# Six more weight granules in the seven-product stage ahead of attention

## The chip, the cores and the metric

One core of one Trainium2 chip runs the whole program. The metric is device time in microseconds of one execution; of several runs the median is given. A profile is one execution, and its times count from the first instruction of the program.

## The reference

The program computes one layer of a hybrid trunk: a half-step feed-forward, token mixing, another half-step feed-forward, over 512 latent and 128 context tokens (640 together) of width 1024. Only the mixing is touched:

```
mq, mk, mv, mo, mg, dq, dk, dv, gm, gd = split_cols(h @ w_in)   # nine projections 1024 wide, gates 16
att = diff_attention(rope(rmsnorm(dq)), rope(rmsnorm(dk)), dv)  # 8 heads, two softmaxes each
hm  = mlstm(mq * 256 ** -0.5, mk, mv, mg)                       # 4 heads of 256, two directions
hm  = rmsnorm(hm) * sigmoid(mo)
y   = sigmoid(gm) * (hm @ w_br_m) + sigmoid(gd) * (att @ w_br_d)
out = y @ w_out
```

Around each half step and the mixing stand modulations: rows of `silu(c) @ w_ada + b`, scaling and shifting the normed tokens and gating the residual.

## The kernel before

**Weights.** A projection 1024 wide is cut into four granules of 256 columns (1 MB each). Every fp32 weight and every activation is split into a high and a low part, and a product is three matmuls (high by high, high by low, low by high). A granule computed directly is four feature units (two column halves by two halves of 320 tokens, 24 matmuls of 320 columns each) or five token units (24 matmuls of 256 columns each).

**The seven-product stage.** `Winograd.products` computes a granule by seven products of half-size blocks in place of eight, 7 x 12 matmuls of 320 columns. ScalarE and VectorE prepare the weights one granule ahead: `parts` makes differences and splits wB and wC, `sums` splits the rest, ww. The order within a granule is A11, S1, the two last products of the granule before, S2, A12, S3. Four results come out per granule: two straight from a bank, two as a bank plus a copy that ScalarE made (`copy_of`). `Gates` runs this stage ahead of attention with six granules: three each of the branch gates gd and gm. Its callback `between(i, at)` does the work that rides along, at the start (0) or late (1) in granule i: the tables of the rotation and the rotation of the first queries and keys.

**Fills.** The other granules are fills. `Fill` holds a queue of granules in a fixed order; TensorE runs one unit of it where the program says so, and ScalarE and VectorE split the next weights. In attention a head has five query blocks. A block writes its scores to a single bank of PSUM, VectorE takes the minimum, ScalarE two exponentials, VectorE mixes the two softmaxes, TensorE transposes the mix in the next block and multiplies by the values. The table `UNITS` says for each head how many units stand in a block behind the transposes (first number) and behind the values (second), and at the head's end. Odd heads end with five further units. Behind the last head `drain(n)` runs units until n granules are left. In the memory stage `fill.pace(us, 1)` spreads the rest over the cells: each cell adds that many us to what is due, and a unit runs when more than 1.4 are due and takes 3.3 off; three units run ahead of the cells.

**Columns.** The 56 column tiles of the later modulations are `Columns`: a tile is a 512 KB load and two multiply-and-sum instructions of VectorE (L813). They ride along in several stages; the memory stage does 12, loaded through SP's queue (`load_columns_raw`).

**Order.** TensorE's instructions stay in the order of the program. On the other engines a planner orders them, except inside `written()`, where the order is that of the program too. DMA queues run in order.

## Time and profile before

| | |
|---|---|
| median of 3 runs | 1818.51 us (1817.56 to 1819.2) |
| span of the profiled execution | 1816.4 us; the page gives no other time for it |
| granted TensorE clock | 1.000 |
| TensorE, VectorE, ScalarE busy | 99%, 73%, 49% of the span |
| seven-product stage | from 505 to 578 us |
| attention | to 1056 us |
| memory stage | to about 1216 us |

In the profile PE is TensorE's matmuls, PEld its weight loads, DVE VectorE, ACT ScalarE, POOL GpSimd and SP the engine that issues most DMAs. A matmul's time is from its start to its modelled end; matmuls overlap, so their pace is read from start to start. ps_f are the banks of seven-product and feed-forward results, ps_p those of feature units, ps_t of token units, sc the scores.

### The profile page before, as it was taken

To read this page: it belongs to the slowest core of one execution; us is meant where nothing else is said; L and a number is where in the kernel's file an instruction comes from. 1 tells how busy PE (TensorE), PEld (TensorE's weight loads), DVE (VectorE), ACT (ScalarE), POOL (GpSimd) and SP (SyncE) were. 2 spreads that over 40 slices of the span, in tenths; PEclk is the share of its full clock that TensorE was granted. 3 is DMA by queue.
4 is the path that set the end of the run, shared out by engine and by line. 5 is a ranking of instruction groups with operands and counts; after the bars stand their busy time and mean duration, and the time that the engine had idled before them with its cause. 6 is when DMAs were issued, how large, how long until landed. Compare 5 with 4: busy or idle time off the path is not lost.

```text
span 1816.4 us, 30813 instructions
## 1 busy us (share of the span) xinstructions
PE 1793.6 (99%) x12622; PEld 1754.8 (97%) x12622; DVE 1323.8 (73%) x2140; ACT 894.8 (49%) x1558; POOL 37.1 (2%) x65
## 2 busy tenths in 40 slices
PE   9999999999999999999999999999999999999998
PEld 7999999999999999999999889999999999999998
DVE  6889986677886776475575649876767888897485
ACT  5654553333755454455465454674336545554432
POOL 0000000100000000000000000000000000000010
PEclk9999999999999999999999999999999999999999
DMA  8255566977244322112222055665652355657992
GB/s 330 106 197 183 185 224 235 344 228 257 82 138 159 106 76 78 63 63 89 80 89 72 20 169 163 223 254 183 238 170 80 134 172 185 202 181 275 352 307 83
DMA packets 130622, 307.69 MB, mean 169 GB/s; under 512 B 9841, under 2 KB 92017, under 8 KB 117553
## 3 DMA queue, kind: packets, MB, share of 16 engines
q1 hardware_dynamic: 120114, 263.64, 42.1%
q0 software_dynamic: 9680, 39.46, 6.7%
q8 instruction: 99, 1.62, 0.4%
q10 hardware_dynamic: 688, 2.63, 0.4%
q14 instruction: 41, 0.34, 0.1%
HBM read 238.14 MB, written 67.56 MB: 168 GB/s over the span
## 4 chain that ended last, share of the span: by engine, by line
PE 84%; DVE 7%; DMA 5%; ACT 3%; issue 1%; SPq 0%; DVEq 0%; ACTq 0%
PE ps_f L75 43%; PE ps_p L75 19%; PE ps_t L75 11%; PE sc L75 3%; PE ps_o L75 2%; DVE ww L54 2%; PE ps_n L75 2%; DMA raw<-in_w2b 2%; DMA raw_a<-in_w_ada_k 1%; PE ps_wT L78 1%; PE ps_u L75 1%; DVE junk L813 1%; PE ps_qkT L78 1%; DMA out_new_c<-Cn 1%; DMA P<-nm_dram 1%
## 5 line engine op out<-in xcount | busy, mean ns | idle before, releaser
L75 PE MATMUL ps_f<-S,ww 128*128 128x320 f32 x2184 | 352.5, 310 | 3.0 <-DMA S<-g_dram 1.0
L75 PEld LDWEIGHTS ps_f<-S,ww 128*128 128x128 f32 x2184 | 327.5, 188 | 7.0 <-DVE ww L54 4.6
L75 PE MATMUL ps_p<-hH,wH 128*128 128x320 f32 x672 | 212.4, 316 | 0.7 <-DVE stage L61 0.7
L75 PE MATMUL ps_p<-hH,wL 128*128 128x320 f32 x672 | 207.7, 309 | 0.0
L75 PE MATMUL ps_p<-hL,wH 128*128 128x320 f32 x672 | 207.7, 309 | 0.0
L54 DVE TENSOR_TENSOR ww<-raw,ww 128x2048 fp32r<-128x2048 f32 (+1 forms) x67 | 150.2, 2241 | 63.7 <-ACT ww L51 63.6
L75 PE MATMUL ps_f<-hm,ww 128*128 128x320 f32 x1176 | 185.8, 309 | 0.6 <-DVE ww L54 0.6
L75 PE MATMUL ps_t<-wH,hH 128*128 128x256 f32 x640 | 185.2, 289 | 0.9 <-DVE x L57 0.9
L75 PE MATMUL ps_t<-wH,hL 128*128 128x256 f32 x640 | 181.0, 283 | 0.9 <-DVE hL L54 0.9
L75 PE MATMUL ps_t<-wL,hH 128*128 128x256 f32 x640 | 180.8, 283 | 0.0
L75 PEld LDWEIGHTS ps_f<-hm,ww 128*128 128x128 f32 x1176 | 175.7, 188 | 1.2 <-DVE ww L54 1.2
L75 PE MATMUL ps_f<-hm,wB 128*128 128x320 f32 x1008 | 161.5, 309 | 0.0
L51 ACT ACTIVATE ww<-raw 128x2048 fp32r<-128x2048 f32 (+1 forms) x67 | 125.3, 1871 | 57.9 <-DVE raw L54 33.6
L75 PEld LDWEIGHTS ps_f<-hm,wB 128*128 128x128 f32 x1008 | 151.3, 188 | 0.0
L54 DVE TENSOR_TENSOR raw<-raw 128x1024 f32<-128x1024 f32 x168 | 145.3, 865 | 1.9
L75 PEld LDWEIGHTS ps_p<-hH,wH 128*128 128x128 f32 x672 | 126.4, 188 | 1.2 <-DVE stage L61 0.9
L75 PEld LDWEIGHTS ps_p<-hL,wH 128*128 128x128 f32 x672 | 126.3, 188 | 0.3
L75 PEld LDWEIGHTS ps_p<-hH,wL 128*128 128x128 f32 x672 | 126.2, 188 | 0.0
L51 ACT ACTIVATE u<-ps_f 128x320 f32<-128x320 f32 x117 | 50.7, 433 | 153.2 <-PE ps_f L75 153.1
L75 PEld LDWEIGHTS ps_t<-wH,hH 128*128 128x128 f32 x640 | 122.3, 191 | 1.5 <-ACT nsq L51 1.1
L75 PEld LDWEIGHTS ps_t<-wH,hL 128*128 128x128 f32 x640 | 122.3, 191 | 1.1 <-DVE hL L54 1.1
L75 PEld LDWEIGHTS ps_t<-wL,hH 128*128 128x128 f32 x640 | 122.5, 191 | 0.4
(307 smaller groups left out, 3444.8 us busy)
## 6 DMA issues: line engine op xcount, KB each, us to landing
g_dram<-g SPq DMA_DIRECT2D x44, 640.0 KB, 7.5
raw_a<-in_w_ada_c POOLq DMA_DIRECT2D x31, 512.0 KB, 4.7
g_dram<-g SPq DMA_DIRECT2D x24, 480.0 KB, 8.2
raw<-in_w1b SPq DMA_DIRECT2D x11, 1024.0 KB, 4.8
raw<-in_w3b SPq DMA_DIRECT2D x11, 1024.0 KB, 6.3
raw<-in_w1a SPq DMA_DIRECT2D x10, 1024.0 KB, 4.9
raw<-in_w3a SPq DMA_DIRECT2D x10, 1024.0 KB, 6.5
hm<-g_dram SPq DMA_DIRECT2D x7, 1280.0 KB, 13.3
```

The costliest lines, as they stand in the source:

```text
L51: return placed(nc.scalar.activation(*args, **kw))
L54: return placed(eng.tensor_tensor(out=out, in0=in0, in1=in1, op=op))
L75: tc.keep_in_program_order(nc.tensor.matmul(*args, **kw))
L78: tc.keep_in_program_order(nc.tensor.transpose(*args, **kw))
L813: placed(vec.tensor_tensor_reduce(out=junk, in0=raw, in1=self.csil[:, v, :], op0=ALU.mult, op1=ALU.add, scale=1.0, scalar=0.0, accum_out=m ...
```

## The change

Six granules leave the fills and join the seven-product stage, which then has twelve: the four output gates mo, and the queries and keys of memory head 0. Their order is four branch gates, mq, mk, four mo, two branch gates. The new results go to DRAM as the branch gates' do; the queries and keys come back into SBUF during attention head 1 (`load_memory`), and the opening of mo (clamp, then exponential of the negative) happens as the results leave PSUM. The scale 1/16 of mq is applied as they leave, and to the copies.

Eight column tiles move from the memory stage to this stage: one each late in granules 5 to 10, one more at the start of granules 8 and 9. Their buffers take the place of those of the rotations, from granule 4 on; they are loaded through POOL's queue (`load_columns`).

The fills are dealt anew: their order, the table `UNITS`, the drain behind the last head (down to 3 granules instead of 5) and the pace of the memory stage (0.8 instead of 1.4).

```diff
@@ copy_of, products
-        def copy_of(self, p, tag, bufs=1):
+        def copy_of(self, p, tag, bufs=1, **kw):
             t = self.tmp.tile([128, HALF], F32, tag=tag, name="u", bufs=bufs)
-            self.copied = act(t, p, AF.Copy)
+            self.copied = act(t, p, AF.Copy, **kw)
...
+                scaled = getattr(gr, "scaled", {})
+                u2 = copy_of(Y, "nacc" if i < 2 * FB - 2 else "nsq", 2, **scaled)
...
+                u3 = copy_of(Y, "nry", **scaled)
@@ fills
+    def load_memory(h):
+        for box, tag, src in ((mqT, "q", mq_dram), (mkT, "k", mk_dram)):
+            box[h] = pair(tag, h, f"m{tag}T")
+            nc.sync.dma_start(out=box[h], in_=src[:, 2 * h : 2 * h + 2, :])
...
     token(project_v(0))
-    open_gate(0, attention)
     values_of(0)
+    values_of(1)
     projections(1)
-    queries_of_memory(0)
-    keys_of_memory(0)
+    queries_of_memory(1)
     token(project_v(1))
-    queries_of_memory(1)
+    keys_of_memory(1)
     projections(2)
-    keys_of_memory(1)
-    values_of(1)
+    values_of(2)
     token(project_v(2))
-    values_of(2)
     projections(3)
-    open_gate(1, attention)
     values_of(3)
+    queries_of_memory(2)
     token(project_v(3))
-    queries_of_memory(2)
     keys_of_memory(2)
     queries_of_memory(3)
     keys_of_memory(3, by_act=True)
-    open_gate(2, memory)
-    open_gate(3, memory)
     gate_unit(a["w_gm"], gm_dram, 3, memory)
     gate_unit(a["w_gd"], gd_dram, 3, memory)
@@ Gates
+            gate = [(a[n], dst, g, self.plain) for g in range(3) for n, dst in (("w_gd", gd_dram), ("w_gm", gm_dram))]
+            rest = [(a["w_mq"], mq_dram, 0, self.query), (a["w_mk"], mk_dram, 0, self.plain)]
+            rest += [(a["w_mo"], o_dram, h, self.opening) for h in range(4)]
+            self.work = []
+            for src, dst, g, f in gate[:4] + rest + gate[4:]:
...
+        def opening(self, t, p, u):
+            if u is None:
+                ts(t, p, -43.0, ALU.max)
+            else:
+                self.at_vec = tt(vec, t, p, u, ALU.add)
+                ts(t, t, -43.0, ALU.max)
+            act(t, t, AF.Exp, scale=-1.0)
@@ between
+        elif (i, at) == (4, 1):
+            early.close()
+            pool = ada.enter_context(tc.tile_pool(name="adag", bufs=1, side="right", reuse_waits="tile"))
+            csil = pool.tile([128, 2, D], F32, name="csil")
+            nc.sync.dma_start(out=csil, in_=csil_dram.partition_broadcast(128))
+            ada_p[:] = pool, pool.tile([128, D], BF16, name="junk")
+            columns.place(len(IN_GATES), csil, load_columns)
+        elif (i, at) in IN_GATES:
+            columns.tile(G.at_vec)
...
+    IN_GATES = [(i, 1) for i in range(5, 11)] + [(i, 0) for i in (8, 9)]
@@ attention
-        0: (two, two, two, two, two, (1, 1, 1)), 1: (two, two, two, one, one, (1,)),
-        2: (two, two, two, two, two, (1, 1, 1)), 3: (two, two, two, one, one, (1,)),
-        4: (two, two, two, two, two, (1, 1, 1)), 5: (two, two, two, two, one, (1,)),
-        6: (one,) * 5 + ((0, 0, 0),), 7: (one,) * 4 + ((0, 0),),
+        0: (two, two, two, two, one, (1, 1, 1)), 2: (two, two, two, one, one, (1, 1, 1)),
+        4: (two, two, two, one, one, (1, 1, 1)),
+        6: (one,) * 5 + ((0, 0, 0),), 7: ((0, 0), one, one, (0, 0), (0, 0), (0, 0)),
     }
+    for hd in (1, 3, 5):
+        UNITS[hd] = two, two, one, one, one, (1,)
...
+            elif (hd, qi) == (1, 0):
+                load_memory(0)
...
-            fill.drain(5)
+            fill.drain(3)
@@ memory
-    fill.pace(1.4, 1)
+    fill.pace(0.8, 1)
...
-    columns.place(12, csil2, load_columns_raw, 1)
+    columns.place(4, csil2, load_columns_raw, 1)
...
-            if n in ((3, 5, 7, 8), (1, 3, 6, 8), (1, 3, 5, 7), ())[h]:
+            if n in ((5,), (3, 7), (5,), ())[h]:
                 columns.tile(m.at_vec)
```

More of the change, by code (lines that the diff above doesn't have):

```diff
@@ L432, in products @@
                 into(Y, S2, False)
-                u2 = copy_of(Y, "nacc" if i < 2 * FB - 2 else "nsq", 2)
+                scaled = getattr(gr, "scaled", {})
+                u2 = copy_of(Y, "nacc" if i < 2 * FB - 2 else "nsq", 2, **scaled)
                 if tail:
@@ L439, in products @@
                 into(Y, S3, False)
-                u3 = copy_of(Y, "nry")
+                u3 = copy_of(Y, "nry", **scaled)
                 if last:
@@ L1330, in tile_trunk @@
     gd_dram = dp.tile([128, KT, T], F32, name="gd_dram")
+    mq_dram = dp.tile([128, KT, T], F32, name="mq_dram")
+    mk_dram = dp.tile([128, KT, T], F32, name="mk_dram")
     qq_dram = dp.tile([128, 2, T], F32, name="qq_dram")
@@ L1671, in finish @@
             nc.sync.dma_start(out=aT_dram[:, self.hd, :], in_=aT)
-    def o_evac(h, pool):
-        def f(p, mt, hf):
-            t = pool.tile([128, HALF], F32, tag="stage", name="stage", bufs=2)
-            ts(t, p, -43.0, ALU.max)
-            act(t, t, AF.Exp, scale=-1.0)
-            nc.sync.dma_start(out=o_dram[:, 2 * h + mt, half(hf)], in_=t)
-        return f
     def gate_evac(dst, g, pool):
@@ L1744, in keys_of_memory @@
         feature(a["w_mk"][h], lambda: k_evac(h, **kw))
-    def open_gate(h, pool):
-        feature(a["w_mo"][h], lambda: o_evac(h, pool()))
     def projections(pr):
@@ L1798, in __init__, with plain, query, done @@
             self.part = {(kh, hf): Of(kh, hf) for kh in range(2) for hf in range(2)}
-            self.work = [
-                [Granule(4, lambda raw, src=src[g]: dma(raw, src)), lambda i: self.ops[i], self.done(dst, g), lambda i: None]
-                for g in range(3) for src, dst in ((a["w_gd"], gd_dram), (a["w_gm"], gm_dram))
-            ]
+            gate = [(a[n], dst, g, self.plain) for g in range(3) for n, dst in (("w_gd", gd_dram), ("w_gm", gm_dram))]
[3 more added lines that the diff above has]
+            for src, dst, g, f in gate[:4] + rest + gate[4:]:
+                gr = Granule(4, lambda raw, src=src[g]: dma(raw, src))
+                if f == self.query:
+                    gr.scaled = dict(scale=0.0625)
+                self.work.append([gr, lambda i: self.ops[i], self.done(dst, g, f), lambda i: None])
         def place_of_fourth(self):
             return self.fp.tile([128, 2, 4, HALF], F32R, tag="s6", name="S")
-        def done(self, dst, g):
+        def plain(self, t, p, u):
+            if u is None:
+                act(t, p, AF.Copy)
+            else:
+                self.at_vec = tt(vec, t, p, u, ALU.add)
+        def query(self, t, p, u):
+            if u is None:
+                act(t, p, AF.Copy, scale=0.0625)
+            else:
+                self.at_vec = stt(t, p, 0.0625, u, ALU.mult, ALU.add)
+        def opening(self, t, p, u):
+            if u is None:
+                ts(t, p, -43.0, ALU.max)
+            else:
+                self.at_vec = tt(vec, t, p, u, ALU.add)
+                ts(t, t, -43.0, ALU.max)
+            act(t, t, AF.Exp, scale=-1.0)
+        def done(self, dst, g, out):
             def f(mt, hf, p, u):
                 t = self.tmp.tile([128, HALF], F32, tag=("nsq", "nt")[mt], name="g_out", bufs=2)
-                if u is None:
-                    act(t, p, AF.Copy)
-                else:
-                    tt(vec, t, p, u, ALU.add)
+                out(t, p, u)
                 nc.sync.dma_start(out=dst[:, 2 * g + mt, half(hf)], in_=t)
@@ L1894, in between @@
             fill.prefetch(0)
+    IN_GATES = [(i, 1) for i in range(5, 11)] + [(i, 0) for i in (8, 9)]
+    ada = ExitStack()
     G.products(G.work, between, narrow=2)
     wide.close()
-    early.close()
+    ada.close()
     right.close()
```

## Prediction

> **What bounds the kernel now.** I began with the page: which engine is never idle, and what the chain of waits ends on.

> ```profile
> span 1816.4 us, 30813 instructions
> PE 1793.6 (99%) x12622; PEld 1754.8 (97%) x12622; DVE 1323.8 (73%) x2140; ACT 894.8 (49%) x1558; POOL 37.1 (2%) x65
> PEclk9999999999999999999999999999999999999999
> PE 84%; DVE 7%; DMA 5%; ACT 3%; issue 1%; SPq 0%; DVEq 0%; ACTq 0%
> ```

> TensorE is busy for 1793.6 of 1816.4 us. So work taken off it is time gained, as long as the places that lose the work do not open holes. The windows by stage (us; then busy time of PE, PEld, DVE, ACT, POOL, granted clock, DMA share, GB/s) are the seven-product stage, attention, the memory stage, and then the first four cells and the four heads of the memory stage:

> ```profile
> 504.00:584.00 80.00, 80.00 (x556) 80.00 (x555) 57.98 (x83) 41.79 (x63) 0.00 (x0) 1.00 0.45 155
> 584.00:1056.00 472.00, 467.96 (x3685) 458.52 (x3684) 288.93 (x440) 242.53 (x498) 0.00 (x0) 1.00 0.22 75
> 1065.00:1216.00 151.00, 148.11 (x875) 135.60 (x874) 125.11 (x368) 93.08 (x238) 0.00 (x0) 1.00 0.61 201
> 1069.44:1078.17 8.73, 7.07 (x33) 5.54 (x31) 4.90 (x13) 4.67 (x16) 0.00 (x0) 1.00 0.84 272
> 1069.44:1100.30 30.86, 29.20 (x165) 25.91 (x164) 25.28 (x78) 17.82 (x49) 0.00 (x0) 1.00 0.43 136
> ```

> Attention has 4.0 us of idle TensorE in 472, the memory stage 2.9 in 151. VectorE is at 61% in attention, 72% in the seven-product stage and 83% in the memory stage.

> **The work removed.** A fill unit is 24 matmuls, a direct weight granule four units or 96 matmuls; by seven products it is 7 x 12 = 84. Their pace is read from a run of twelve in the timeline, and from the five units that follow one another at the end of head 7:

> ```profile
> 523.71 1.92 PE L75 MATMUL ps_f<-S,ww 128*128 128x320 f32 x12
> 1036.46:1054.14 17.68, 17.68 (x121) 17.58 (x120) 0.98 (x2) 1.31 (x3) 1.00 0.16 60
> ```

> The twelve start (1.92 - 0.31)/11 = 0.146 us apart, 0.31 us being what a single one shows; five units take 17.68 us, 3.53 each. Six granules change place, so 6 x 12 x 0.146 = **10.5 us** of TensorE work goes. A granule takes 84 x 0.146 = 12.3 us in the stage; attention loses 16 units (106 to 90 by the table of units, the drain counted) and the memory stage 8 (20 to 12).

> A lone unit also pays for the switch from other matmuls:

> ```profile
> 1010.31 0.39 PE L75 MATMUL ps_p<-hH,wH 128*128 128x320 f32 x1
> 1010.54 0.30 PE L75 MATMUL ps_p<-hL,wH 128*128 128x320 f32 x1
> 1010.68 0.31 PE L75 MATMUL ps_p<-hH,wL 128*128 128x320 f32 x1
> ```

> The second starts 0.23 us after the first, not 0.146. Of the 24 units five stood in a row; 19 x 0.08 = **-1.6 us**. And one wait of the stretch ahead of attention goes, where a unit waited for VectorE to empty an output gate's bank; value projections, emptied by ScalarE, now stand there: **-0.7 us** (between 0 and that).

> ```profile
> PE ps_p L75 <- DVE stage L61: 0.7, 1, 0.7
> ```

> **Where the fills covered something.** The new table gives head 7 nothing at blocks 0, 3 and 4 (block 4 had nothing before), and the drain behind the last head, which ran five units, has none left. Block 0, on TensorE, VectorE and ScalarE:

> ```profile
> 1003.27 0.30 PE L75 MATMUL ps_p<-hH,wH 128*128 128x320 f32 x1
> 1006.79 0.71 PE L78 MATMUL ps_aT<-ident,ao 128*128 128x128 f32 x5
> 1008.17 0.50 PE L75 MATMUL sc<-kH,qT 128*128 128x512 f32 x1 [0.68 <-ACT p L51]
> 1004.46 1.75 DVE L1614 TENSOR_REDUCE mn<-sc 128x2 f32<-128x1536 f32 x1
> 1007.92 0.20 ACT L51 ACTIVATION_READ_ACCUMULATOR p<-sc,mn 128x1 f32 x1
> ```

> The score bank is single. The next scores at 1008.17 wait until the second exponential has read it (1007.92 + 0.20), which waits for the minimum, which VectorE starts at 1004.46 behind the work of head 6's end; none of that changes. With the unit at 1003.27 the block already ended in a wait, so without it the block is not shorter: the unit's **3.5 us** were free here and are paid elsewhere. Block 3:

> ```profile
> 1022.07 0.47 PE L75 MATMUL sc<-kH,qT 128*128 128x512 f32 x1
> 1027.22 0.20 ACT L51 ACTIVATION_READ_ACCUMULATOR p<-sc,mn 128x1 f32 x1
> 1028.34 1.01 DVE L57 SCALAR_TENSOR_TENSOR p<-p,r,p 128x768 f32<-128x768 f32 x1
> 1028.98 0.36 PE L75 MATMUL sc<-kH,qT 128*128 128x256 f32 x1
> ```

> From scores to scores 6.91 us. Without its unit the bank is free at 5.35, but the transposes behind the next scores (0.7 us on) wait for the mixing, which can end at about 6.9 (1.01 after some 0.5 of small steps behind 1027.42). So the block counts as some 6.2: it gains 0.7 of 3.5, a loss of **2.8 us** (2.0 by the bank alone). Behind head 7:

> ```profile
> 1036.32 0.38 PE L75 MATMUL ps_o<-v_tok,wT 128*128 128x128 f32 x2
> 1041.06 0.82 DVE L54 TENSOR_TENSOR ao<-ao,ry 128x640 f32<-128x640 f32 x1
> 1054.14 0.71 PE L78 MATMUL ps_aT<-ident,ao 128*128 128x128 f32 x5
> ```

> The last head's norm runs from 1036.7 to 1041.88, 0.9 of it behind two evacuations that leave. The five units hid it; now TensorE, which keeps its order, stands still for **4.3 us** (to 5.2) ahead of the transposes, and the first three units of the memory stage come behind them. Together +10.6: what the products save.

> The other blocks that go from two units to one (nine of them) cost nothing: with a token unit (256 columns for 320, so some 2.9 us for 3.53) a block like block 3 takes 6.91 - 0.6 = 6.3 us, against 5.35 to the freed bank.

> **What VectorE gets.** Its rows of the seven-product stage, a column tile's and an output gate's clamp, then two pairs of granules of the first half step, where the same column tiles ride along:

> ```profile
> L54 DVE TENSOR_TENSOR raw<-raw 128x512 f32<-128x512 f32 (+1 forms) x15 | 13.0, 866 | 0.2
> L54 DVE TENSOR_TENSOR ww<-raw,ww 128x2048 fp32r<-128x2048 f32 x5 | 11.4, 2289 | 5.2 <-ACT ww L51 5.2
> L54 DVE TENSOR_TENSOR wB<-raw,wB 128x1024 fp32r<-128x1024 f32 x5 | 6.1, 1219 | 0.0
> L54 DVE TENSOR_TENSOR wC<-raw,wC 128x512 fp32r<-128x512 f32 x5 | 3.4, 683 | 0.0
> L54 DVE TENSOR_TENSOR g_out<-ps_f,u 128x320 f32<-128x320 f32 x11 | 5.3, 485 | 3.2 <-PE ps_f L75 3.2
> L813 DVE CUSTOM_DVE_ANT_0 raw_a<-raw_a,csil 128x1024 bf16<-128x1024 f32 x24 | 29.1, 1212 | 0.0
> L61 DVE TENSOR_SCALAR stage<-ps_p 128x320 f32<-128x320 f32 x8 | 3.9, 488 | 0.8 <-PE ps_p L75 0.7
> 198.40:223.00 24.60, 24.48 (x168) 24.22 (x167) 22.25 (x31) 12.37 (x19) 0.53 (x1) 1.00 0.60 202
> 247.60:272.20 24.60, 24.43 (x165) 23.91 (x164) 23.09 (x35) 11.24 (x17) 1.06 (x2) 1.00 0.69 249
> ```

> A granule costs (13.0 + 11.4 + 6.1 + 3.4)/5 + 2 x 0.49 = 7.8 us. A tile adds 2 x 1.2, with its small reads 2.6; an output gate four clamps of at most 0.49, 1.9. Against 12.3 us: granules 6 and 7 come to 12.3; granules 8 and 9, with two tiles each, to 14.9, over by 5.2 in all, made good in 10 (10.4) and 11 (no weights to prepare). At 90 to 94% the first half step loses 0.1 to 0.2 us of TensorE per pair. Weights are prepared a granule ahead, and the last part of them (ww) is wanted only at the second product, 1.8 us into the next granule, which I reckon as some 3 us of slack: **+0.5 us**, between 0 and 5.2. The tile loads move from SP's queue to POOL's; the one load of the conditioning rows, new on SP, waits for the end of the rotations and holds up weight loads that are wanted a granule later. The 8 stores and 2 loads of head 0's queries and keys are spread over SP and wanted much later: nothing.

> In heads 1 and 3 the rotation of the next pair falls later against the packing that needs it:

> ```profile
> 653.00:665.00 12.00, 11.80 (x107) 11.66 (x106) 9.35 (x18) 7.84 (x17) 0.00 (x0) 1.00 0.25 89
> 665.00:699.30 34.30, 34.30 (x253) 33.45 (x252) 27.82 (x35) 20.41 (x38) 0.00 (x0) 1.00 0.22 72
> ```

> These 46.3 us hold 37.2 of VectorE. The key projection now ends two units nearer to head 1 (6 us) and its blocks up to the packing take 29 us, not 34.3: 35 us are left for 35 to 37. Packing is late by 0 to 2.3 us per head, ScalarE's copies queue behind it, and TensorE has some 3 us in hand there: **+0.5** (0 to 4.6).

> **The memory stage** loses 8 of 20 units and 8 tiles (8 x 2.6 = 21 us of VectorE), so VectorE falls to about 78% of a shorter stage. Its pace falls from 1.4 to 0.8, so the first fill comes behind the twelfth cell, the second of head 1, instead of behind the sixth. The first four cells, without a fill, hold 1.66 us of idle TensorE, 0.42 each, as the window shows; I take **+0.5** (from -2.9, all idle time of the stage gone, to +5.4, below).

> **Sum:** -10.5 - 1.6 - 0.7 + 3.5 + 2.8 + 4.3 + 0.5 + 0.5 + 0.5 = -0.7 on a span of 1816.4. The median of the three runs is 1818.51, 2.1 above the span; with that, 1817.8. What a measurement of this kernel can tell from no change is 0.2%, 3.6 us.

> **Rivals.**
> 1. Faster: VectorE's new loads cost nothing, and the memory stage, relieved of its tiles, loses its 2.9 us of idle time. -12.8 + 10.6 - 2.9 = -5.1: 1813.4. For it: 94% of VectorE hardly stops the first half step. Against: the memory stage's waits stand at its start, where no tile ran. 0.27.
> 2. Slower: the memory stage's cells run without cover. If each of the 17 cells of its first two heads that no fill follows idles as the first four do, that is 7.1 us against 1.66, +5.4 in place of 0.5: 1822.7. It decides from 4 us of added idle time there. Against: behind the first four cells head 0 has next to none, fills or not. 0.15.
> 3. Slower: VectorE's 5.2 us in granules 8 and 9 come through whole: 1822.5. 0.05.
> 4. Slower: the holes lower the granted clock. Every row above reads 1.00, but no hole of 4 us stands in them. If the clock were halved behind the holes at block 0 and behind head 7 for as long as they last, 8.5 us: 1826.3. 0.03.

> [...]

> **How the numbers follow.** The forecast, no change, has 0.50. Faster is rival 1, 0.27; slower rivals 2 to 4, 0.23. The range goes from 1812.5, just past rival 1, to 1824, past rivals 2 and 3; what is left out is rival 4 and the bounds of several terms at once.

> **What would show it.** Right: the seven-product stage some 74 us longer with TensorE full; blocks 0 and 3 of head 7 at 6.7 and about 5.4 to 6.2 us with waits for ScalarE and VectorE; 4 us of idle TensorE ahead of the last head's transposes; attention some 46 us shorter, the memory stage some 28. Wrong: no hole at head 7, waits for ww beyond 2 us in granules 8 to 10, ScalarE waiting for the rotated queries in head 1, or a granted clock below 1.

## The result, and the profile after

The changed kernel takes **1838.73 us** (median of 4 runs, 1835.84 to 1840.45) against 1818.57 for the kernel before on the same chip: ratio 1.0112 [1.0099, 1.0125], slower by 20 us where 0.7 us faster was forecast. It lies outside the range and beyond the worst of the rivals, 1826.3.

The page of the changed kernel: span, the engines' busy time, and the shares of the chain of waits.

```profile
span 1835.8 us, 30811 instructions
PE 1791.9 (98%) x12550; PEld 1749.2 (95%) x12550; DVE 1350.7 (74%) x2178; ACT 909.8 (50%) x1588; POOL 41.3 (2%) x73
PE 83%; DVE 9%; DMA 4%; ACT 3%; issue 1%; SPq 0%; DVEq 0%; ACTq 0%
```

12622 - 12550 = 72 matmuls have gone, as worked out, but the span is 19.4 us longer: the difference is time in which TensorE stands still or runs slowly. The windows by stage of the changed kernel (us; busy PE, PEld, DVE, ACT, POOL; granted clock, DMA share, GB/s) say where: the seven-product stage, attention with the units ahead of it, the memory stage.

```profile
505.00:658.00 153.00, 150.24 (x1021) 149.24 (x1020) 124.79 (x177) 74.29 (x114) 4.23 (x8) 1.00 0.53 180
658.00:1100.00 442.00, 421.79 (x3338) 410.11 (x3337) 276.09 (x427) 232.89 (x487) 0.00 (x0) 0.99 0.22 72
1109.50:1232.00 122.50, 117.95 (x667) 105.05 (x666) 95.78 (x315) 80.82 (x210) 0.00 (x0) 1.00 0.49 158
```

TensorE idles 2.8 us in the stage (0.0 before), 20.2 in attention (4.0 before) and 4.6 in the memory stage (2.9 before), and the clock of attention is no longer 1.00.

**Head 7.** TensorE's rows in the timeline, with the idle time before each and who ended it: block 0 and its late transposes, the scores of blocks 1 to 4, the last head's transposes and the first fill behind them.

```profile
1055.43 0.49 PE L75 MATMUL sc<-kH,qT 128*128 128x512 f32 x1 [0.23 <-DVE kH L1593]
1058.73 0.74 PE L78 MATMUL ps_aT<-ident,ao 128*128 128x128 f32 x5 [1.26 <-DVE ao L54]
1062.21 0.79 PE L75 MATMUL sc<-kH,qT 128*128 128x512 f32 x1 [2.74 <-ACT p L51]
1071.87 0.47 PE L75 MATMUL sc<-kH,qT 128*128 128x512 f32 x1
1078.78 0.47 PE L75 MATMUL sc<-kH,qT 128*128 128x512 f32 x1
1084.18 0.38 PE L75 MATMUL sc<-kH,qT 128*128 128x256 f32 x1 [1.03 <-ACT p L51]
1097.28 1.30 PE L78 MATMUL ps_aT<-ident,ao 128*128 128x128 f32 x5 [4.31 <-DVE ao L54]
1098.91 0.47 PE L75 MATMUL ps_p<-hH,wL 128*128 128x320 f32 x1
1099.18 0.47 PE L75 MATMUL ps_p<-hH,wH 128*128 128x320 f32 x1
```

Block 0 takes 6.78 us with no unit in it, as it did with one; block 3 takes 5.40; the hole behind the head is 4.31. These are the forecast's figures. But block 1, with the same work as before, takes 9.66 us where it took 6.99, and the matmuls of the first fill start 0.27 us apart, not 0.146. The windows of 3.41 us each around the two holes show why:

```profile
1054.50:1057.91 3.41, 2.64 (x15) 1.66 (x14) 2.76 (x9) 2.17 (x6) 0.00 (x0) 1.00 0.00 0
1057.91:1061.32 3.41, 0.74 (x5) 0.53 (x5) 2.34 (x2) 1.92 (x5) 0.00 (x0) 1.00 0.04 14
1061.32:1064.73 3.41, 2.52 (x8) 2.23 (x9) 1.40 (x3) 0.84 (x2) 0.00 (x0) 0.50 0.24 87
1064.73:1068.15 3.42, 3.42 (x15) 3.22 (x15) 1.76 (x1) 2.05 (x5) 0.00 (x0) 0.50 0.00 0
1092.04:1095.45 3.41, 0.93 (x7) 0.74 (x6) 1.34 (x3) 1.38 (x3) 0.00 (x0) 1.00 0.00 0
1095.45:1098.86 3.41, 1.58 (x7) 1.61 (x8) 1.32 (x4) 0.66 (x2) 0.00 (x0) 0.50 0.00 0
1098.86:1102.28 3.42, 3.42 (x14) 3.42 (x14) 1.10 (x1) 2.29 (x3) 0.00 (x0) 0.50 0.56 170
```

Behind each hole the granted clock is 0.50 for 6.83 us, two such windows.

**Head 3.** Its window before, then after; then, of the changed kernel, the last step of the next pair's rotation on VectorE, ScalarE's packing copy, the minimum of block 4 behind the packing on VectorE, ScalarE's copy of the turned probabilities, and the value product that waits for it.

```profile
787.00:847.70 60.70, 60.60 (x485) 59.56 (x484) 41.91 (x61) 31.50 (x62) 0.00 (x0) 1.00 0.24 80
```

```profile
849.90:910.50 60.60, 55.83 (x460) 54.21 (x459) 39.70 (x62) 31.06 (x68) 0.00 (x0) 1.00 0.21 71
...
884.64 1.22 DVE L54 TENSOR_TENSOR q_tok<-q_tok,rope 128x1024 f32<-128x1024 f32 x1
...
885.89 0.74 ACT L51 ACTIVATE qpk<-q_tok 128x640 fp32r<-128x640 f32 x1
...
887.40 0.42 DVE L1617 TENSOR_REDUCE mn<-sc 128x2 f32<-128x256 f32 x1
...
887.79 0.85 ACT L51 ACTIVATE wT<-ps_wT 128x512 f32<-128x512 f32 x2
888.42 1.60 PE L75 MATMUL ps_o<-v_tok,wT 128*128 128x128 f32 x12 [3.02 <-ACT wT L51]
```

The head idles 4.8 us against 0.1. The copy starts 0.03 us after the rotation ends (885.86), and what stands behind it on ScalarE is what TensorE needs. In head 1 the same chain idles 2.1 us; there ScalarE itself stands still until the rotated queries come:

```profile
772.47 0.74 ACT L51 ACTIVATE qpk<-q_tok 128x640 fp32r<-128x640 f32 x1 [2.63 <-DVE q_tok L54]
```

**The stage and the memory stage.** VectorE's sum for ww in granule 9's weights and the product that wants it; then TensorE's waits in each of the two stages (line, releaser: total, times, longest).

```profile
614.47 2.29 DVE L54 TENSOR_TENSOR ww<-raw,ww 128x2048 fp32r<-128x2048 f32 x1 [0.50 <-ACT ww L51]
...
616.81 1.00 PE L75 MATMUL ps_f<-S,ww 128*128 128x320 f32 x5 [1.32 <-DVE ww L54]
...
PE ps_f L75 <- DVE ww L54: 2.6, 2, 1.3
...
PE ps_u L75 <- ACT wv L51: 2.0, 2, 1.4
PE ps_u L75 <- DVE C L57: 1.9, 1, 1.9
```

There are four candidates, then: the holes of head 7 themselves, the half clock behind them, VectorE in granules 8 and 9, and the late rotation. Each got a run that takes it away, the holes together with the half clock behind them.

### The profile page after: what moved, and what is told of

It reads as the page before. It is cut to its first block, busy times and chain, and to the rows that moved or that the text cites. A ratio compares the mean times of both kernels' runs of the same rounds, so it can differ in the third digit from the quotient of the medians.

```text
span 1835.8 us, 30811 instructions
## 1 busy us (share of the span) xinstructions
PE 1791.9 (98%) x12550; PEld 1749.2 (95%) x12550; DVE 1350.7 (74%) x2178; ACT 909.8 (50%) x1588; POOL 41.3 (2%) x73
## 4 chain that ended last, share of the span: by engine, by line
PE 83%; DVE 9%; DMA 4%; ACT 3%; issue 1%; SPq 0%; DVEq 0%; ACTq 0%
PE ps_f L75 48%; PE ps_p L75 14%; PE ps_t L75 11%; PE sc L75 2%; PE ps_o L75 2%; DVE ww L54 2%; DMA raw_a<-in_w_ada_k 1%; PE ps_wT L78 1%; PE ps_qkT L78 1%; DVE junk L814 1%; DMA raw<-in_w2b 1%; PE ps_n L75 1%; DMA out_new_c<-Cn 1%; DVE mn L1617 0%; PE ps_u L75 0%
## 5 line engine op out<-in xcount | busy, mean ns | idle before, releaser
L75 PE MATMUL ps_f<-S,ww 128*128 128x320 f32 x2400 | 388.1, 310 | 6.2 <-DVE ww L54 3.0
L75 PEld LDWEIGHTS ps_f<-S,ww 128*128 128x128 f32 x2400 | 359.8, 188 | 11.4 <-DVE ww L54 8.2
L54 DVE TENSOR_TENSOR ww<-raw,ww 128x2048 fp32r<-128x2048 f32 (+1 forms) x73 | 163.9, 2245 | 66.9 <-ACT ww L51 66.8
L75 PE MATMUL ps_t<-wH,hH 128*128 128x256 f32 x640 | 185.2, 289 | 0.9 <-DVE x L57 0.9
L75 PE MATMUL ps_f<-hm,ww 128*128 128x320 f32 x1176 | 185.8, 309 | 0.1
L75 PE MATMUL ps_t<-wH,hL 128*128 128x256 f32 x640 | 181.0, 283 | 0.9 <-DVE hL L54 0.9
L75 PE MATMUL ps_t<-wL,hH 128*128 128x256 f32 x640 | 180.8, 283 | 0.0
L75 PEld LDWEIGHTS ps_f<-hm,ww 128*128 128x128 f32 x1176 | 175.7, 188 | 0.5 <-DVE ww L54 0.5
L51 ACT ACTIVATE ww<-raw 128x2048 fp32r<-128x2048 f32 (+1 forms) x73 | 136.8, 1874 | 57.1 <-DVE raw L54 33.0
L54 DVE TENSOR_TENSOR raw<-raw 128x1024 f32<-128x1024 f32 x186 | 160.7, 864 | 2.2
L75 PE MATMUL ps_f<-hm,wB 128*128 128x320 f32 x1008 | 161.5, 309 | 0.0
L75 PE MATMUL ps_p<-hH,wH 128*128 128x320 f32 x480 | 152.6, 318 | 0.7 <-DVE y L54 0.7
L75 PEld LDWEIGHTS ps_f<-hm,wB 128*128 128x128 f32 x1008 | 151.3, 188 | 0.0
L75 PE MATMUL ps_p<-hL,wH 128*128 128x320 f32 x480 | 149.4, 311 | 0.0
L75 PE MATMUL ps_p<-hH,wL 128*128 128x320 f32 x480 | 149.4, 311 | 0.0
L51 ACT ACTIVATE u<-ps_f 128x320 f32<-128x320 f32 x129 | 55.8, 433 | 162.2 <-PE ps_f L75 161.9
L75 PEld LDWEIGHTS ps_t<-wH,hH 128*128 128x128 f32 x640 | 122.3, 191 | 1.4 <-ACT nsq L51 1.1
L75 PEld LDWEIGHTS ps_t<-wH,hL 128*128 128x128 f32 x640 | 122.3, 191 | 1.1 <-DVE hL L54 1.1
L75 PEld LDWEIGHTS ps_t<-wL,hH 128*128 128x128 f32 x640 | 122.5, 191 | 0.3
L54 DVE TENSOR_TENSOR wL<-raw,wH 128x2048 fp32r<-128x2048 f32 x37 | 84.7, 2288 | 22.9 <-ACT wH L51 22.7
L1617 DVE TENSOR_REDUCE mn<-sc 128x2 f32<-128x1536 f32 (+1 forms) x40 | 59.6, 1489 | 56.9 <-PE sc L75 56.7
L814 DVE CUSTOM_DVE_ANT_0 junk<-raw_a,csil 128x1024 bf16<-128x1024 f32 (+1 forms) x78 | 95.0, 1217 | 6.3 <-DMA raw_a<-in_w_ada_c 5.8
```

What stands on the lines that cost most here:

```text
L51: return placed(nc.scalar.activation(*args, **kw))
L54: return placed(eng.tensor_tensor(out=out, in0=in0, in1=in1, op=op))
L75: tc.keep_in_program_order(nc.tensor.matmul(*args, **kw))
L814: placed(vec.tensor_tensor_reduce(out=junk, in0=raw, in1=self.csil[:, v, :], op0=ALU.mult, op1=ALU.add, scale=1.0, scalar=0.0, accum_out=m ...
L1617: placed(vec.tensor_reduce(out=mn, in_=sv, axis=AX.X, op=ALU.min))
```

## The experiments

All ratios are to the kernel before, timed on the same chip; idle times are a window's length less its busy PE; the changed kernel's is 1.0112 [1.0099, 1.0125].

**The clock alone.** Matmuls that nobody reads, into a free bank, at the two holes.

```diff
             if late is not None:
+                if hd == 7:
+                    idle(4)
                 late()
                 late = None
+                if hd == 7:
+                    idle(11)
...
             fill.drain(3)
+            idle(16)
```

> The changed kernel with 31 matmuls of 128 columns whose result nobody reads, into a free bank, at the two places of head 7 where TensorE stands still: 4 ahead of and 11 behind the late transposes of block 0, 16 ahead of the last head's transposes. They give no work and fill no wait whole; all else is the same. Theory A (the holes themselves are waits on VectorE, and what the trace shows beyond them, two stretches of 6.83 us with a granted clock of 0.50, is a second price): the two half-clock stretches go, the mean granted clock is 1.000, block 1 of head 7 takes 7.0 us instead of 9.65, the units behind the last head lose some 2.3 us: 4 to 6 us faster than the changed kernel, about 1833.5. Rival B (the low clock in the record costs nothing, since those stretches wait for other engines anyway): within 1 us of the changed kernel. Rival C (the added matmuls stand in the way): 2 to 3 us slower.

1835.80 us, ratio 1.0102 [1.0085, 1.0118]: 1.8 us faster by the ratios, with intervals that overlap. The profile is clearer. Scores of blocks 1 and 2 of head 7 in the timeline of this run:

```profile
1063.11 0.50 PE L75 MATMUL sc<-kH,qT 128*128 128x512 f32 x1 [0.29 <-ACT p L51]
...
1070.10 0.47 PE L75 MATMUL sc<-kH,qT 128*128 128x512 f32 x1
```

Block 1 takes 6.99 us, 2.67 less. No half clock is left there, as the window over head 7 shows, and no added matmul made a head longer:

```profile
1056.30:1096.80 40.50, 35.43 (x255) 32.38 (x255) 20.04 (x38) 17.27 (x44) 0.00 (x0) 1.00 0.02 9
```

From the first scores of attention to the memory stage's first transposes this run is 3.8 us shorter. From there to the last cell the same instructions take 2.0 us more, which says nothing of the edit: in the four profiles with these same instructions (this one, the changed kernel, and two of the runs below) the stretch takes 119.0 to 122.8 us. (The profile also has a half clock of 3.41 us among the first loads, at 34 us, far from the edit.) So A holds for the place (3.8 us); its whole-run figure of 4 to 6 is not shown, since the times differ by 1.8 us only, within overlapping intervals.

**How short a hole is enough.** The same, with only the 4 matmuls ahead of block 0's late transposes.

> The changed kernel with only the 4 unread matmuls ahead of the late transposes of head 7's block 0; the 11 behind them and the 16 behind the head are left out, so an idle stretch of 2.9 us and one of 4.5 us remain. If the clock is halved by an idle stretch of about 3.4 us: block 1 of head 7 takes 7.0 us (no half clock there), and the units behind the last head still run at half. If any hole of some 3 us is enough, block 1 stays at 9.65 us. 2.5 us faster than the changed kernel by the first, the same by the second.

One run, 1840.55 us. Block 1 takes 8.33 us, between the two forecasts, and one half clock stands ahead of it and one in it. Windows of 3.41 us of this run around block 0:

```profile
1053.89:1057.30 3.41, 2.52 (x22) 1.89 (x20) 3.41 (x7) 2.35 (x6) 0.00 (x0) 1.00 0.05 22
1057.30:1060.72 3.42, 3.34 (x12) 3.05 (x13) 2.77 (x7) 0.72 (x4) 0.00 (x0) 0.50 0.00 0
1060.72:1064.13 3.41, 1.06 (x10) 0.82 (x8) 0.96 (x1) 2.42 (x5) 0.00 (x0) 1.00 0.20 72
1064.13:1067.54 3.41, 3.07 (x10) 2.58 (x11) 1.51 (x4) 0.29 (x2) 0.00 (x0) 0.50 0.08 29
```

The first reading falls: with a hole of 2.7 us (2.69 by the timeline) the clock is halved all the same, behind a window that still holds 1.06 us of work, and once more ahead of the hole, behind a window with 2.52 us of which 2.02 are the transposes of queries and keys. Such windows of several runs stand together further down.

**The holes filled.** Head 7's units back; four of the memory stage's twelve units pay for them.

```diff
-        6: (one,) * 5 + ((0, 0, 0),), 7: ((0, 0), one, one, (0, 0), (0, 0), (0, 0)),
+        6: (one,) * 5 + ((0, 0, 0),), 7: (one, one, one, one, (0, 0), (0, 0)),
...
-            fill.drain(3)
+            fill.drain(2)
```

> The changed kernel with head 7's fills as before (a unit at each of blocks 0 to 3 in front of the values) and two units drained behind the last head's values: four units leave the memory stage's start for the holes. Theory A (the fills taken from head 7 were the loss there: head 7 is 14.2 us poorer against its work, of which some 5 are the half clock): 10 to 15 us faster than the changed kernel, 1824 to 1829, no half clock. The memory stage pays back part of it, since its pace now runs out of units earlier: up to 4 us. Rival B (the units were free in the memory stage, and moving them is neutral): within 2 us of the changed kernel, with the waits found again in the memory cells.

1836.25 us, ratio 1.0103 [1.0088, 1.0118]: nothing gained by the time. Attention holds four units more, 14 us, at an unchanged length (413.6 us from the first scores to the last transposes, after 412.7), so the holes are gone, as A says; but the memory stage now ends without a fill. Its end in this run, the window and the wait:

```profile
1225.00:1240.00 15.00, 4.18 (x21) 3.92 (x20) 5.85 (x19) 13.37 (x21) 0.00 (x0) 0.63 0.92 342
...
PE ps_hT L78 <- DVE hs L57: 10.8, 1, 10.8
```

The last memory head's norm, which the last units had hidden, stands open for 10.8 us, with a half clock of 13.65 us that begins in this hole. A's 4 us for the memory stage was too little. That is rival B's outcome in the time and not its reason: moved units were free where they came to and dear where they came from.

**The column tiles back.** All twelve in the memory stage, none among the granules.

```diff
-        elif (i, at) in IN_GATES:
-            columns.tile(G.at_vec)
...
-    columns.place(4, csil2, load_columns_raw, 1)
+    columns.place(12, csil2, load_columns_raw, 1)
...
-            if n in ((5,), (3, 7), (5,), ())[h]:
+            if n in ((3, 5, 7, 8), (1, 3, 6, 8), (1, 3, 5, 7), ())[h]:
```

> The changed kernel with all twelve column tiles in the memory stage, at the places they have in the kernel before, and none in the seven-product stage. Theory A (the two waits of 1.49 us for ww and the smaller ones, 3.8 us in all, come from the tiles' 2.4 us each in granules 8 and 9): the stage's idle TensorE falls from 3.8 to under 0.5 us and the stage to 148 us; the memory stage gets 0 to 4 us longer, its VectorE having 21 us more in a stage without the cover of 8 units. In all between 4 us faster and 1 us slower. Rival B (the waits come from the granules' own preparation, two granules of output gates following one another): the waits of 1.49 us stay, and the time is the changed kernel's or more.

1847.91 us, ratio 1.0167 [1.0149, 1.0185]. The stage and the memory stage of this run:

```profile
505.00:654.00 149.00, 149.00 (x1020) 149.00 (x1020) 107.08 (x143) 74.67 (x114) 0.00 (x0) 1.00 0.43 149
...
1106.50:1242.30 135.80, 121.38 (x682) 106.86 (x681) 113.56 (x352) 82.49 (x217) 0.00 (x0) 1.00 0.56 183
```

The stage is full and 3.8 us shorter (attention starts 4.3 us earlier, but 0.5 of that lies ahead of the stage): the tiles are the whole of the stage's loss. But the memory stage idles 14.4 us against 4.6. With 20 units it carried twelve tiles at 2.9 us of idle time; with 12 units it doesn't. The forecast of A for the memory stage, 0 to 4 us, was wrong; the tiles' move, taken by itself, is a gain.

**The rotation earlier.** Two lines of the list of fills change places.

```diff
-    keys_of_memory(1)
     projections(2)
+    keys_of_memory(1)
```

> The changed kernel with the third pair's key and query projections four units earlier in the list of fills (the second head's memory keys behind them instead of ahead). Theory A (head 3 loses 5.3 us because the rotation of the third pair, which begins when its last projection is evacuated, is on VectorE past the point where the packing for head 4 wants it): the idle TensorE of 3.18 and 1.58 us about head 3 is gone, head 3 is 4 to 5 us shorter: about 1834. Rival B (VectorE is simply full there, 46 us with the rotation in it, so the place does not matter): the wait moves to an earlier block of heads 2 and 3 and the time stays within 1.5 us of the changed kernel.

1830.58 us, ratio 1.0074 [1.0059, 1.0089], 6.9 us faster than the changed kernel by the ratios. Head 3's window and ScalarE's packing copy in this run:

```profile
850.60:907.90 57.30, 57.22 (x460) 55.94 (x459) 36.20 (x59) 27.43 (x62) 0.00 (x0) 1.00 0.24 83
...
881.04 0.74 ACT L51 ACTIVATE qpk<-q_tok 128x640 fp32r<-128x640 f32 x1
```

Idle time falls from 4.8 us to 0.1. The copy starts 30.4 us into the head instead of 36.0. Heads 2 and 3 together are 4.9 us shorter, and no other head changes by more than 0.2. A holds, B falls; what the times gain beyond 5 us lies in the memory stage (1.8 us), whose instructions are the same.

**All four mended.** The same twelve granules; tiles one to a granule from 5 on, with a second one in granule 5; projections earlier; four units from heads 2 and 3 for head 7.

```diff
-    keys_of_memory(1)
     projections(2)
     values_of(2)
     token(project_v(2))
     projections(3)
+    keys_of_memory(1)
     values_of(3)
+    token(project_v(3))
     queries_of_memory(2)
-    token(project_v(3))
...
+        0: (two, two, two, two, two, (1, 1, 1)), 2: (two, one, one, one, one, (1, 1, 1)),
...
+        6: (one,) * 5 + ((0, 0, 0),), 7: (one, one, one, one, (0, 0), (0, 0)),
...
+    UNITS[1] = two, two, one, one, one, (0,)
+    UNITS[3] = one, one, one, one, one, (1,)
...
-    IN_GATES = [(i, 1) for i in range(5, 11)] + [(i, 0) for i in (8, 9)]
+    IN_GATES = [(i, 1) for i in range(5, 11)] + [(5, 0), (11, 0)]
```

> The same twelve granules and eight tiles, dealt once more: two tiles of granules 8 and 9 go to granules 5 and 11; the third pair's projections come nine units earlier and the fourth's four earlier against the last values (second head's memory keys in heads 4 and 5, the third's queries in heads 6 and 7); heads 2 and 3 give up four units, and head 7 has a unit at blocks 0 to 3 again and two drained behind its last values; head 1 gets one unit less and head 0 one more. Twelve units stay in the memory stage. Theory A (the four places found so far are the whole loss): against the changed kernel the stage gains some 4 us, head 3 some 5, head 1 some 2, head 7 some 9 and the clock some 4: 1812 to 1817, at or below the kernel before, all idle places named gone. Rival B (what is taken out of one place opens the next, since VectorE and ScalarE have no more time per block): the waits come back in heads 2 and 3, whose blocks now have one unit, and the time stays above 1822.

1818.94 us, ratio 1.0010 [1.0001, 1.0019]: 18.5 us of the 20 are back by the ratios. Stage and attention of this run, and two windows of 3.41 us in head 3:

```profile
505.00:655.50 150.50, 148.84 (x1015) 148.35 (x1014) 123.46 (x175) 73.92 (x114) 4.23 (x8) 1.00 0.54 182
655.50:1085.00 429.50, 419.31 (x3335) 407.81 (x3334) 275.80 (x427) 232.53 (x487) 0.00 (x0) 1.00 0.22 74
...
866.15:869.56 3.41, 1.74 (x13) 1.34 (x12) 2.02 (x6) 3.41 (x7) 0.00 (x0) 1.00 0.12 38
869.56:872.97 3.41, 3.41 (x17) 3.41 (x17) 2.46 (x7) 2.25 (x8) 0.00 (x0) 0.50 0.00 0
```

The time lies between A's figure and B's. Attention idles 10.2 us instead of 20.2, so B is half right: the blocks of heads 2 and 3, now with one unit each, wait, and behind one such wait the clock reads 0.50 again, for 3.41 us. TensorE still waits once for ww, 1.6 us at 590.9, in granule 7: the two tiles of granule 5 have slid back, and three tiles run on VectorE between the sums of ww for granules 6 and 7 (576.0 and 590.8).

**The memory stage's waits.** On top of the last kernel, two instructions that wait for DMAs put further back on their engines.

```diff
-              for d in range(2):
-                tt(vec, self.P[:, :, d, :], self.P[:, :, d, :], mask[:, d, None, :].to_broadcast([128, 5, 128]), ALU.add)
...
+            later[2].append(lambda: mem[h + 1].masked(m.at_vec))
...
+            with tc.issue_after(self.at_vec.ins):
+                act(self.so, self.so, AF.Ln, bias=1.0)
```

> The kernel with the fills dealt once more, and in the memory stage two instructions that wait for transfers put further back on their engines: the mask additions of the next head's decay rows behind that head's third cell instead of at the head's start, and the logarithm of the output gate behind the head's last cell. Theory A (the memory stage's two long waits of TensorE, 2.02 and 1.52 us, are VectorE and ScalarE standing at these two for a DMA, with a cell's work queued behind): the stage gets 2.5 to 4 us shorter than with the fills dealt alone. Rival B (the cells have no cover, and any order leaves the same idle time): within 1 us.

1823.32 us, ratio 1.0030 [1.0018, 1.0042], slower than without. From the first cell to the last the stage takes 120.0 us instead of 115.9. TensorE's longest waits are now for VectorE's C ahead of the numerators:

```profile
PE ps_n L75 <- DVE C L57: 2.7, 2, 1.5
```

Neither theory said this. That the two waits were the stage's loss is not shown; they have moved, and the order before was the better one.

**One granule given back.** Eleven granules; the last output gate is again four direct units of the memory stage, and heads 2 and 3 keep theirs. Block 0 of head 1 has both its units ahead of the late transposes. Seven tiles in the stage, five in the memory stage. Several things change at once here, so the granule's own worth is not separated.

```diff
+    open_gate(3, memory)
     gate_unit(a["w_gm"], gm_dram, 3, memory)
...
+    UNITS[1] = (2, 0), two, one, one, one, (0,)
...
-            rest += [(a["w_mo"], o_dram, h, self.opening) for h in range(4)]
+            rest += [(a["w_mo"], o_dram, h, self.opening) for h in range(3)]
```

> The fills dealt once more, with one granule given back: the last output gate is a direct granule of the memory stage again, so eleven granules stay in the seven-product stage and 106 direct units are there. Heads 2 to 5 keep their 24 units a pair, with the third pair's projections four units earlier; heads 6 and 7 take twelve; block 0 of head 1 has both its units ahead of the late transposes; seven tiles in the stage, one to a granule from granule 5 on and two in the last, five in the memory stage. Theory A (the four units that heads 2 and 3 gave up, 9.7 us idle there with a half clock of 3.41 us, were dearer than the 1.75 us that a direct granule takes more): idle 3 us in heads 2 and 3, no wait for ww of over 1 us in the stage, about 6 us faster than with the fills dealt alone: 1811 to 1814, below the kernel before. Rival B (a direct granule costs as much as it covers): 1817 to 1820.

1817.33 us, ratio 0.9989 [0.9980, 0.9999]. The stage has no wait for ww, and heads 2 and 3 idle as little as foretold; but head 1 has a new wait of 2.35 us with a half clock behind it (from 642 to 1081 us the granted clock is 0.99):

```profile
759.58 0.84 PE L78 MATMUL ps_wT<-ident,p 128*128 128x128 f32 x6 [2.35 <-DVE p L57]
```

(The expectations count a wait from where the next matmul would have started, 0.16 us more.) So the 6 us of A became some 3.8 by the ratios, and the time itself lies in B's range: A's waits went, its figure did not come.

**Head 1 again.** Its block 0 back at one unit ahead of the late transposes and one behind.

> The kernel with eleven granules, with block 0 of head 1 back at one unit ahead of the late transposes and one behind them; nothing else differs. Theory A (with both units ahead, the small steps of the rotation fall later against the packing in head 1, and the wait of 2.51 us with its half-clock stretch of 3.41 us is the price): head 1 takes 58.5 us instead of 60.1, with waits of 1.58 us at the late transposes and 0.84 us at the packing, and no half clock there: 1 to 3 us faster, about 1815.5. Rival B (the rotation is late by the count of units ahead of it, which stays the same): within 0.5 us.

1817.42 us, ratio 0.9992 [0.9982, 1.0001]: the same as the last run within what can be measured. In its profile head 1 is 1.6 us shorter, 58.5 us, and its half clock is gone, as A says (from 644 to 1081 us the granted clock is 1.00); the time shows none of A's 1 to 3 us and is the one that B gives. Stage, attention and memory stage of this run:

```profile
505.00:644.00 139.00, 138.88 (x945) 138.20 (x944) 115.17 (x160) 67.99 (x104) 3.70 (x7) 1.00 0.54 181
644.00:1081.00 437.00, 431.87 (x3445) 421.89 (x3444) 278.21 (x429) 236.17 (x492) 0.00 (x0) 1.00 0.22 75
1090.00:1215.00 125.00, 119.66 (x670) 105.17 (x670) 99.95 (x325) 83.45 (x223) 0.00 (x0) 1.00 0.53 171
```

Idle TensorE is 0.1, 5.1 and 5.3 us, 10.6 in all (0.1 + 5.13 + 5.34); the kernel before has 6.9, the changed one 27.5. The best of these versions is about 0.1% faster than the kernel before, which a measurement of this kernel hardly tells from no change.

## Why the prediction was wrong

The direction of nearly every term was right, and the size of the ones called 0.5 was not. By stages: the seven-product stage became 77.7 us longer and not full (74 and full was forecast), attention 35.1 us shorter from its first turns to the last head's transposes (46; 31.6 of it from the first scores on), the memory stage 25.2 (28). Two of the four signs named for a wrong forecast are there: ScalarE waits for rotated queries, and the clock is below 1. ww is late too, but by 1.3 us at a time and not by the 2 that were named.

- **Work removed, -10.5.** 72 matmuls went. The two small gains, -1.6 for lone units and -0.7 for the bank that VectorE emptied, were not tested; the row of that wait is gone from the stretch ahead of attention.
- **Head 7 and the drain, +10.6.** Right: block 0 keeps its 6.78 us, block 3 takes 5.40 with waits of 1.03 and 0.8 us for the next block (5.4 to 6.2 was forecast), the hole is 4.31 us (4.3).
- **Granted clock: left out of the sum, rival 4 with a chance of 0.03.** This is the step that failed in kind. "Every row above reads 1.00, but no hole of 4 us stands in them" was the reason to leave it out; it was the reason to put it in, since the forecast's own terms made two such holes. The run with unread matmuls puts its price at 3.8 us up to the memory stage. Rival 4's 8.5 us is the length of both holes; at half clock for that long (matmuls 0.27 us apart, not 0.146) at most half of it, 4.3, is lost, so the rival was priced at twice what its condition gives; 4.3 is near the 3.8.
- **Rotation, +0.5 (0 to 4.6).** "Packing is late by 0 to 2.3 us per head ... and TensorE has some 3 us in hand." The mechanism was the right one. Counted from where the next matmul would have started, and with the short waits, TensorE lost some 5.3 us more in head 3 than before and 2.4 in head 1, 7.7 together; putting the projections four units earlier takes head 3's away. The share of VectorE over a stretch of 46 us hid that packing, the next minimum and the copies of the turned probabilities stand in line behind the last rotation step, so TensorE's spare time had ended before they came. Head 3 was given head 1's figure without a row of its own.
- **VectorE in the stage, +0.5 (0 to 5.2).** The run without tiles gives 3.8, near the upper end. "Some 3 us of slack" was not there when granules 8 and 9 needed it: ww is summed last in VectorE's line, and for granule 6 the sum ends only 0.5 us ahead of its product, with tiles (577.0 and 577.5) and without (576.5 and 577.0). Without tiles this lead grows to 4.5 us by granule 9 (609.4 and 613.9); with them it stays at 1.1 us or less, and ww is 1.3 us late in granules 9 and 10. The sum over a granule isn't the condition, the arrival of ww is.
- **Memory stage, +0.5 (-2.9 to 5.4).** 3.0: it became 25.2 us shorter, and 8 x 3.53 = 28.2 were taken out. Within the bounds. With twelve tiles it would have been far worse (14.4 us idle), so rival 2's mechanism is real and the tiles' move is what held it down.

The misses add up: 3.8 + 7.2 + 3.3 + 2.5 = 16.8 of the 20.1 us between forecast and result (span 19.4 longer, -0.7 forecast). 3.3 are not placed; 1.0 of them lies ahead of the seven-product stage, where both kernels have the same instructions and where all eleven profiles differ by up to 3.2 us. The 2.5 of the memory stage is no firmer than the spread of that stage given above. No single rival was the result. The range was drawn past rivals taken one at a time, and the terms that were chosen near the low end of their bounds all depended, as far as the runs show, on one thing: how much of VectorE's and ScalarE's time had been covered by the units that left.

## What to carry to other kernels

A fill on a saturated engine did two things here: it cost its own time, some 3.5 us a unit, and it covered the others' latency, as the 4.31 us behind head 7 show. Price a removed fill by the block that it leaves, from the arrival of the operand that the block waits for next, and not by the share of a stage. Where a change opens several stretches without cover, take their bounds together, and count the half clock behind each, here 6.83 us behind either hole of head 7. And when a move saves little per piece (1.75 us for a granule here), a version that moves fewer pieces can be worth more: eleven granules, dealt with more care, did no worse than twelve.

## What the runs showed of the hardware

**The window ahead of it.** The 3.41 us ahead of these stretches were not idle. They held this much TensorE work: 0.74 and 0.93 us in the changed kernel, 1.74 with all four mended, and 0.20, 1.06, 1.38, 1.59 and 2.52 with only the 4 matmuls. Windows with as much work as some of these were followed by full clock. Counted in the steps given above, outside the stretches at half, every window with 1.56 us or more was in the changed kernel, and every one with 2.01 us or more in the kernel before. In the changed kernel one about the wait in head 3 held 1.56 us (883.83 to 887.24), and one in the memory stage as much, the stage's clock being 1.00 throughout:

```profile
1139.79:1143.21 3.42, 1.56 (x9) 1.01 (x7) 1.28 (x3) 0.19 (x1) 0.00 (x0) 1.00 0.75 224
```

In the window of 2.52 us, the one at 1053.89 above, 2.02 us were transposes, but that alone does not decide it. In the changed kernel this window, with 2.54 us of such transposes in it, was followed by full clock (1054.50 above):

```profile
1051.08:1054.50 3.42, 2.78 (x31) 2.66 (x31) 2.49 (x5) 1.87 (x5) 0.00 (x0) 1.00 0.42 137
```

What sets the window of 2.52 us apart stays open.

**Its end.** Of the windows at half clock, those with 1.58 and 2.52 us of TensorE work in the changed kernel, and the one with 2.42 us with only the 4 matmuls, were followed by another at 0.50; those with 3.07 to 3.42 us, of both kernels, by one at 1.00. The holes of head 7 in the changed kernel reach into the first halved window, and behind each of them two windows were at half.

**The same instructions at both clocks.** Five of the profiles have head 3 of the changed kernel unaltered. In the changed kernel itself and in the run with unread matmuls the clock stayed at 1.00 there. With only the 4 matmuls it was 0.50 from 886.64 to 893.47 us, behind a window with 1.38 us of work; with the holes filled and with the column tiles back it was 0.62 (888 to 892 us) and 0.63 (884 to 888 us). So the half clock in head 3 came in three of the five executions.
